# Grouping the mLSTM read-out by kind of matmul, and summing the dense feed-forward on VectorE with the residual at group 8

## The chip, the cores and the metric

The kernel runs on one core of one Trainium2 chip. The metric is the device time of one execution in microseconds (us); the time before is the median of three runs. TensorE multiplies matrices out of SBUF into PSUM, VectorE, ScalarE and GpSimd work on tiles element by element, and SyncE issues most transfers between HBM and SBUF. The engines run side by side, each through its own list of instructions in a fixed order, and wait for each other by semaphores.

## The reference

The model has two layers over 512 tokens (x) and 256 context tokens (ctx) of width 1024. Each layer mixes tokens by two recurrences side by side, HGRN2 and mLSTM, in both directions, and then applies a feed-forward: layer 0 a dense one, layer 1 a mixture of 8 experts of which each token takes two. A row `mod` of six modulation vectors comes from `w_ada`. Cut to what the change touches:

```python
# mLSTM, per chunk and head (one direction; both are summed)
s   = einsum("bhid,bhjd->bhij", qc, kc) * exp(d - m[..., None])
num = einsum("bhij,bhjv->bhiv", s, vc) + w_inter * einsum("bhid,bhdv->bhiv", qc, c_prev)
den = sum(s, -1) + w_inter[..., 0] * einsum("bhid,bhd->bhi", qc, n_prev)
h   = num / maximum(abs(den), exp(-m))[..., None]
...
# layer 0, feed-forward (D_FF = 2816), on x and on ctx
f = (silu(h @ w_gate) * (h @ w_up)) @ w_down
x = layer_norm(ALPHA * x + mod[:, 5] * f, ln_g, ln_b)
```

## The kernel before

Tokens lie on the 128 partitions: four tiles of x and two of ctx, together 768 tokens. Matmuls of weights run in a split form: each fp32 weight piece is loaded into a raw buffer (tag `wr`, two of them), ScalarE copies its rounded high part to `wh` (line 134), VectorE subtracts it and writes the low part `wl` (line 140, in the token mix shared with GpSimd in line 138), and `mm3` multiplies three times (lines 172 to 174). The activations have high and low parts as well (`xh`, `xl`, `hh`, `hl`).

**Read-out of the mLSTM.** The kernel's chunks have 128 tokens, ten passes over the two layers. For a chunk, line 726 makes scores of queries and keys (64 rows, since a head has 64 channels; even heads lie in rows 0 to 63, odd heads in 64 to 127), VectorE multiplies them by the decays into `W` (tile `tmp`), and the read-out adds for each of 4 heads and 2 directions the product of `W` with the values (line 736, 128 rows, 129 columns: the last column is the denominator) and the product of the queries with the state before the chunk (line 738, 64 rows). Both directions of a head share a PSUM tile of the tag "o", of which there are two; ScalarE copies a finished tile to `num` (line 739). These matmuls are in fp32, and the trace shows each as two records.

**Dense feed-forward of layer 0.** D_FF is cut into 11 groups of 256 columns, numbered 0 to 10. In each group the gate and up products are made in columns of hidden units, multiplied (line 865 and the lines behind it give `s`, `hh`, `hl`), and the down product of the six token tiles and two halves of 512 columns makes twelve PSUM tiles, in turn of the tags "o" and "sc", two buffers each. `evac` takes each of them into the accumulator `pre`: group 0 by a copy on ScalarE, each later one by a product with the modulation row `bd` on VectorE (line 1006) into a buffer `xm`, and a sum on GpSimd (line 1012). Groups 9 and 10 share one down product, so there is no evacuation at group 9; the last one sums on VectorE. In group 1, `evac` also multiplies what group 0 left by the row (line 1010) and adds the residual, which line 1009 loads from HBM into a buffer `xr` (line 1011). `xm` and `xr` take turns in four buffers of one tag. Between the groups, in groups 0 to 6, stand sums over `w_ada` for the next layer's modulation (lines 330 and 332: VectorE, pieces of 1024 columns that SyncE loads into `ar`).

The order on every engine is set when the program is built, by a scheduler that takes the instructions by priority as their inputs and buffers come free; names such as `o_1555` are its tiles.

Of the kernel before, what the change touches and what calls it, by code (L numbers as in the profile page):

```python
# [7 lines left out]
F32 = mybir.dt.float32  # L8
# [3 lines left out]
AF = mybir.ActivationFunctionType  # L12
OP = mybir.AluOpType
PSUM = bass.MemoryType.PSUM

P = 128
# [11 lines left out]
D_FF = 2816  # L28
# [21 lines left out]
class Kern:  # L50
# [483 lines left out]
    def mlstm(self, l, xh, xl, last):  # L534

        nc = self.nc
# [3 lines left out]
        for i in range(2):  # L540
            s = self.slot([3, 4, 129], True)
            nc.vector.memset(s[:, :, :, 128:129], 1.0)
            va.append(s)
        VA = lambda c: va[c // 3][:, c % 3]
        wmv = [self.w_cols(w, O_MV + 256 * half, 256) for half in range(2)]
        for t in range(NT):
            for half in range(2):
                p = self.gemm_T(wmv[half], xh, xl, t, 256)
# [8 lines left out]
        for f in range(2):  # L557
            for d in range(2):
                o = lambda t: t[:, :, 32 * f + 4 * d:32 * f + 4 * d + 4]
# [3 lines left out]
        for t0, n in ((0, TX), (TX, TC)):  # L563
            p = self.gemm_F((gh, gl), 0, 40, xh, xl, t0, n)
# [90 lines left out]
        for half, o in ((0, O_MQ), (1, O_MK)):  # L655
# [3 lines left out]
            for b in range(2):  # L659
                kcol = 2 * half + b  # L660
                for t0, n, seg in ((0, TX, 64), (TX, TC, TC)):
                    if last and half == 0 and t0:
                        continue
                    p = self.gemm_F(wqk, b * P, P, xh, xl, t0, n)
# [12 lines left out]
        st = lambda d, c: inc[c // 3][:, c % 3, 2 * d:2 * d + 2]  # L677
        for c in range(NT):
# [7 lines left out]
            for d in range(2):  # L686
# [3 lines left out]
                for hd in range(4):  # L690
                    b, s = hd // 2, hd % 2
                    nc.tensor.matmul(pc[64 * s:64 * s + 64, b], kw[:, d, hd], VA(c)[:, hd], start=True, stop=True)
                nc.scalar.activation(st(d, c), pc, AF.Copy)
        for i in range(1, NT - 1):
            for d in range(2):
                c, cp = ORDER[d][i], ORDER[d][i - 1]
# [3 lines left out]
        for c in (range(NX) if last else ORDER[0]):  # L700
            ds = [d for d in range(2) if POS[d][c] > 0]
# [5 lines left out]
            qs = self.s4([2, 2, P])  # L707
            for s in range(2):
                r = slice(64 * s, 64 * s + 64)
# [6 lines left out]
            W = M  # L716
# [4 lines left out]
            for s in range(2):  # L721

                pq = self.psum("sc", [P, 2, P])
                r = slice(64 * s, 64 * s + 64)
# [3 lines left out]
                    wv = W[:, d].rearrange("p (b s) t -> p b s t", s=2)[:, :, s]  # L728
                    nc.vector.tensor_tensor(wv, pq, wv, OP.mult)
            num = self.shp(self.sp.tile([P, 1032], F32, tag="num", name=self.nm("num"), bufs=2), [2, 4, 129])  # L730
            for hd in range(4):
                b, s = hd // 2, hd % 2
                r = slice(64 * s, 64 * s + 64)
                pn = self.psum("o", [P, 2, 129])
                for d in range(2):
                    nc.tensor.matmul(pn[:, d], W[:, d, hd], VA(c)[:, hd], start=True, stop=d not in ds)
                    if d in ds:
                        nc.tensor.matmul(pn[:, d], qs[r, d, b], st(d, ORDER[d][POS[d][c] - 1])[r, b], start=False, stop=True)
                nc.scalar.activation(num[:, :, hd], pn, AF.Copy)
            den = self.sp.tile([P, 2, 4], F32, tag="den", name=self.nm("den"), bufs=2)  # L740
            dv = num[:, :, :, 128]
            nc.vector.scalar_tensor_tensor(den, dv, -1.0, dv, op0=OP.mult, op1=OP.max)
# [161 lines left out]
    def run(self):  # L904
        nc, I, tc = self.nc, self.I, self.tc
# [23 lines left out]
        for l in range(DEPTH):  # L929
# [29 lines left out]
            for nqs in ((0,), (1,), (2, 3)):  # L959
# [4 lines left out]
                for t in range(nt):  # L964
                    for nq, w in zip(nqs, ww):
                        p = self.gemm_T(w, xh, xl, t, 256)
                        c = slice(nq * 256, nq * 256 + 256)
# [31 lines left out]
            def evac(t, half, p, g, end):  # L999
                c = slice(512 * half, 512 * half + 512)  # L1000
                o, bd = pre[:, t, c], bc5[t // NX][:, c]
                if g == 0:
                    nc.scalar.activation(o, p, AF.Copy)
                    return
                m = self.lp.tile([P, 512], F32, tag="xr", name=self.nm("xm"), bufs=4)
                nc.vector.tensor_tensor(m, p, bd, OP.mult)  # L1006
                if g == 1:
                    xr = self.lp.tile([P, 512], F32, tag="xr", name=self.nm("xr"), bufs=4)
                    nc.sync.dma_start(xr, self.xd[t * P:(t + 1) * P, c])
                    nc.vector.tensor_tensor(o, o, bd, OP.mult)  # L1010
                    nc.vector.scalar_tensor_tensor(o, xr, ALPHA, o, op0=OP.mult, op1=OP.add)
                (nc.vector if end else nc.gpsimd).tensor_tensor(o, o, m, OP.add)  # L1012

            def finish(t):
                self.finish(pre[:, t], self.stats(pre[:, t]), self.xd[t * P:(t + 1) * P], gb)
# [556 lines left out]
        return O, Wt  # L1572


PREP = 3
STREAMS = ((0, 1, 2), (6, 3, 7, 4, 5))
LEAD = 0.95
# [5 lines left out]
ORDER = ([4, 5, 0, 1, 2, 3], [5, 4, 3, 2, 1, 0])  # L1583
POS = [{c: i for i, c in enumerate(o)} for o in ORDER]
# [22 lines left out]
```

## Time and profile before

| | us |
|---|---|
| three runs | 2311.2, 2299.89, 2292.64 |
| median | 2299.89 |
| the profiled execution | 2313.89 |
| its span in the trace | 2312.1 |
| TensorE busy in it | 2093.4 (91%) |
| VectorE busy | 1530.9 (66%) |
| ScalarE busy | 912.4 (39%) |
| GpSimd busy | 526.8 (23%) |

The rows quoted further down are of the profiled execution, with times from the start of its span. The granted clock of TensorE (PEclk) is a share of its full 2.4 GHz; its mean over the span was 0.947. The first layer's token mix comes first, the dense feed-forward runs from about 640 to 1220 us, then come the second layer's token mix and its experts.

### The profile page before, as it was taken

To read this page: it belongs to the slowest core of one execution; us is meant where nothing else is said; L and a number is where in the kernel's file an instruction comes from. 1 tells how busy PE (TensorE), PEld (TensorE's weight loads), DVE (VectorE), ACT (ScalarE), POOL (GpSimd) and SP (SyncE) were. 2 spreads that over 40 slices of the span, in tenths; PEclk is the share of its full clock that TensorE was granted. 3 is DMA by queue.
4 is the path that set the end of the run, shared out by engine and by line. 5 is a ranking of instruction groups with operands and counts; after the bars stand their busy time and mean duration, and the time that the engine had idled before them with its cause. 6 is when DMAs were issued, how large, how long until landed. Compare 5 with 4: busy or idle time off the path is not lost. (4 is left out here: it accounts for less than half of the span.)

```text
span 2312.1 us, 32153 instructions
## 1 busy us (share of the span) xinstructions
PE 2093.4 (91%) x12225; PEld 1771.5 (77%) x12225; DVE 1530.9 (66%) x2527; ACT 912.4 (39%) x1443; POOL 526.8 (23%) x389
## 2 busy tenths in 40 slices
PE   8999999897799999999997999999979899798991
PEld 3887688897777777888886887889967787576781
DVE  4374684858977877544338366867669677776774
ACT  3334333344332221121124345334337565765661
POOL 1111312324621334443308112222220000000003
PEclk9998999998999999999998999999969999899996
DMA  7121311246354565222122222122558778888885
GB/s 256 39 87 43 118 44 44 71 143 202 128 161 145 174 191 158 65 64 64 55 68 75 61 77 69 42 60 80 205 181 296 237 266 280 264 282 274 280 283 133
DMA packets 232360, 333.38 MB, mean 144 GB/s; under 512 B 14608, under 2 KB 181716, under 8 KB 232200
## 3 DMA queue, kind: packets, MB, share of 16 engines
q1 hardware_dynamic: 228504, 319.14, 42.8%
q0 software_dynamic: 3696, 12.13, 2.1%
q8 instruction: 98, 1.61, 0.3%
q14 instruction: 62, 0.51, 0.1%
HBM read 305.98 MB, written 25.24 MB: 143 GB/s over the span
## 5 line engine op out<-in xcount | busy, mean ns | idle before, releaser
L173 PE MATMUL g<-xl,wh 128*128 128x512 f32 (+1 forms) x1168 | 402.1, 344 | 5.5 <-DVE xl L391 5.5
L174 PE MATMUL g<-xh,wl 128*128 128x512 f32 (+1 forms) x1168 | 401.7, 344 | 2.8 <-DVE wl L140 2.8
L172 PE MATMUL g<-xh,wh 128*128 128x512 f32 (+1 forms) x1168 | 402.7, 345 | 1.2 <-DVE s L865 0.9
L134 ACT ACTIVATE wh<-wr 128x1024 fp32r<-128x1024 f32 x240 | 249.2, 1055 | 253.5 <-PE sc L174 102.5
L172 PE MATMUL g<-wh,xh 128*128 128x256 f32 x1024 | 299.4, 293 | 19.6 <-DVE pre L968 11.2
L173 PE MATMUL g<-wl,xh 128*128 128x256 f32 x1024 | 298.0, 292 | 4.9 <-DVE wl L138 3.2
L174 PE MATMUL g<-wh,xl 128*128 128x256 f32 x1024 | 295.5, 289 | 0.0
L140 DVE TENSOR_TENSOR wl<-wr,wh 128x1024 fp32r<-128x1024 f32 x176 | 233.3, 1340 | 66.6 <-ACT wh L134 57.3
L173 PEld LDWEIGHTS g<-xl,wh 128*128 128x128 f32 x1168 | 221.6, 190 | 33.2 <-DVE xl L391 6.0
L172 PEld LDWEIGHTS g<-xh,wh 128*128 128x128 f32 x1168 | 221.7, 190 | 30.3 <-DVE s L865 1.3
L174 PEld LDWEIGHTS g<-xh,wl 128*128 128x128 f32 x1168 | 221.6, 190 | 30.3 <-DVE wl L140 4.1
L1012 POOL TENSOR_TENSOR pre<-pre,xm 128x512 f32<-128x512 f32 x96 | 159.5, 1691 | 330.4 <-DVE xm L1006 229.1
L157 DVE TENSOR_TENSOR wl<-wr,wh 128x1024 fp32r<-128x1024 f32 x154 | 186.1, 1219 | 53.8 <-ACT wh L156 52.5
L172 PEld LDWEIGHTS g<-wh,xh 128*128 128x128 f32 x1024 | 199.0, 195 | 24.9 <-DVE pre L968 11.8
L173 PEld LDWEIGHTS g<-wl,xh 128*128 128x128 f32 x1024 | 198.7, 194 | 7.5 <-DVE wl L138 3.9
L174 PEld LDWEIGHTS g<-wh,xl 128*128 128x128 f32 x1024 | 198.4, 194 | 0.7 <-issue 0.6
L156 ACT ACTIVATE wh<-wr 128x1024 fp32r<-128x1024 f32 x154 | 161.2, 1055 | 76.1 <-DMA wr<-in_moe_w_gate_up 65.4
L138 POOL TENSOR_TENSOR wl<-wr,wh 128x384 fp32r<-128x384 f32 x64 | 90.5, 1424 | 328.3 <-ACT wh L134 293.4
L332 DVE SCALAR_TENSOR_TENSOR acc<-ar,cond,acc 128x1024 f32<-128x1024 f32 x77 | 115.9, 1516 | 28.6 <-DMA ar<-in_w_ada 28.6
L138 DVE TENSOR_TENSOR wl<-wr,wh 128x640 fp32r<-128x640 f32 x64 | 66.4, 1039 | 90.2 <-ACT wh L134 89.4
L865 DVE TENSOR_TENSOR s<-g,s 128x512 f32<-128x512 f32 (+1 forms) x44 | 24.4, 553 | 129.0 <-PE g L174 129.0
L866 ACT ACTIVATE hh<-s 128x512 fp32r<-128x512 f32 (+1 forms) x44 | 23.0, 523 | 185.6 <-DVE s L865 185.6
(480 smaller groups left out, 4377.5 us busy)
## 6 DMA issues: line engine op xcount, KB each, us to landing
wr<-in_moe_w_gate_up SPq DMA_DIRECT2D x176, 512.0 KB
wr<-in_moe_w_down SPq DMA_DIRECT2D x88, 512.0 KB
wr<-in_w_in SPq DMA_DIRECT2D x64, 512.0 KB
ar<-in_w_ada SPq DMA_DIRECT2D x64, 512.0 KB
wr<-in_ffn_w_gate_up SPq DMA_DIRECT2D x44, 512.0 KB
wr<-in_w_ada SPq DMA_DIRECT2D x32, 512.0 KB
wr<-in_ffn_w_down SPq DMA_DIRECT2D x22, 512.0 KB
wr<-in_w_out SPq DMA_DIRECT2D x16, 512.0 KB
```

Source lines behind the costliest of these rows:

```text
L134: nc.scalar.activation(fl(h), r, AF.Copy)
L138: eng.tensor_tensor(fl(lo)[:, sl], r[:, sl], fl(h)[:, sl].bitcast(F32), OP.subtract)
L140: nc.vector.tensor_tensor(fl(lo), r, fl(h).bitcast(F32), OP.subtract)
L156: nc.scalar.activation(v(h, u), r, AF.Copy)
L157: nc.vector.tensor_tensor(v(lo, u), r, v(h, u).bitcast(F32), OP.subtract)
L172: nc.tensor.matmul(out, ah, bh, start=(i == 0), stop=False)
L173: nc.tensor.matmul(out, ah, bl, start=False, stop=False)
L174: nc.tensor.matmul(out, al, bh, start=False, stop=(i == n - 1))
L332: nc.vector.scalar_tensor_tensor(o, wk, cs, o, op0=OP.mult, op1=OP.add)
L865: nc.vector.tensor_tensor(s, pu, s, OP.mult)
L866: nc.scalar.activation(hh[:, b, t0:t0 + n], s, AF.Copy)
L1012: (nc.vector if end else nc.gpsimd).tensor_tensor(o, o, m, OP.add)
```

## The change

Two edits. In the read-out, two heads of a pair (`s` = 0 and 1) are taken together: both PSUM tiles of the tag "o", first the four products with `W`, then the products with the state, those of the two halves of rows next to each other, then both copies. In the dense feed-forward, groups 1 to 8 add the PSUM tile to the accumulator on VectorE, without the row and without GpSimd; the row is multiplied in, and the residual loaded and added, once, in group 8 (`GRES`). The last evacuation (groups 9 and 10) multiplies by the row and sums on VectorE as before.

```diff
             num = self.shp(self.sp.tile([P, 1032], F32, tag="num", name=self.nm("num"), bufs=2), [2, 4, 129])
-            for hd in range(4):
-                b, s = hd // 2, hd % 2
-                r = slice(64 * s, 64 * s + 64)
-                pn = self.psum("o", [P, 2, 129])
-                for d in range(2):
-                    nc.tensor.matmul(pn[:, d], W[:, d, hd], VA(c)[:, hd], start=True, stop=d not in ds)
-                    if d in ds:
-                        nc.tensor.matmul(pn[:, d], qs[r, d, b], st(d, ORDER[d][POS[d][c] - 1])[r, b], start=False, stop=True)
-                nc.scalar.activation(num[:, :, hd], pn, AF.Copy)
+            for b in range(2):
+                pn = [self.psum("o", [P, 2, 129]) for _ in range(2)]
+                for s in range(2):
+                    for d in range(2):
+                        nc.tensor.matmul(pn[s][:, d], W[:, d, 2 * b + s], VA(c)[:, 2 * b + s], start=d == 0, stop=False)
+                for d in ds:
+                    for s in range(2):
+                        r = slice(64 * s, 64 * s + 64)
+                        nc.tensor.matmul(pn[s][:, d], qs[r, d, b], st(d, ORDER[d][POS[d][c] - 1])[r, b],
+                                         start=False, stop=d == ds[-1])
+                for s in range(2):
+                    nc.scalar.activation(num[:, :, 2 * b + s], pn[s], AF.Copy)
...
                 if g == 0:
                     nc.scalar.activation(o, p, AF.Copy)
                     return
-                m = self.lp.tile([P, 512], F32, tag="xr", name=self.nm("xm"), bufs=4)
-                nc.vector.tensor_tensor(m, p, bd, OP.mult)
-                if g == 1:
+                if end:
+                    m = self.lp.tile([P, 512], F32, tag="xr", name=self.nm("xm"), bufs=4)
+                    nc.vector.tensor_tensor(m, p, bd, OP.mult)
+                    nc.vector.tensor_tensor(o, o, m, OP.add)
+                    return
+                nc.vector.tensor_tensor(o, p, o, OP.add)
+                if g == GRES:
                     xr = self.lp.tile([P, 512], F32, tag="xr", name=self.nm("xr"), bufs=4)
                     nc.sync.dma_start(xr, self.xd[t * P:(t + 1) * P, c])
                     nc.vector.tensor_tensor(o, o, bd, OP.mult)
                     nc.vector.scalar_tensor_tensor(o, xr, ALPHA, o, op0=OP.mult, op1=OP.add)
-                (nc.vector if end else nc.gpsimd).tensor_tensor(o, o, m, OP.add)
...
+GRES = D_FF // 256 - 3
```

After the change the lines behind 739 have moved by five. What the scheduler makes of it shows in the order of the instructions.

TensorE, read-out of a chunk in layer 0, the first three heads before the change (`early`, `tmp`: operands of the product with `W`; `s`: the state):

```order
L736 MATMUL o_1555<-early_421,tmp_1525 128x129 [waits DMAHW0_49,DVE_49]
L738 MATMUL o_1555<-tmp_1209,s_207_1528 128x129
L736 MATMUL o_1555<-early_421,tmp_1525 128x129 [waits DMAHW1_49,DVE_49]
L738 MATMUL o_1555<-tmp_1209,s_207_1528 128x129
L736 MATMUL o_1561<-early_421,tmp_1525 128x129 [waits DVE_49]
L738 MATMUL o_1561<-tmp_1209,s_207_1528 128x129
L736 MATMUL o_1561<-early_421,tmp_1525 128x129 [waits DVE_49]
L738 MATMUL o_1561<-tmp_1209,s_207_1528 128x129
L736 MATMUL o_1567<-early_421,tmp_1525 128x129 [waits Activation_49]
```

The same place after it:

```order
L737 MATMUL o_1555<-early_421,tmp_1525 128x129 [waits DMAHW0_49,DVE_49]
L737 MATMUL o_1555<-early_421,tmp_1525 128x129 [waits DMAHW1_49,DVE_49]
L737 MATMUL o_1556<-early_421,tmp_1525 128x129 [waits DVE_49] x2
L741 MATMUL o_1555<-tmp_1209,s_207_1528 128x129
L741 MATMUL o_1556<-tmp_1209,s_207_1528 128x129
L741 MATMUL o_1555<-tmp_1209,s_207_1528 128x129
L741 MATMUL o_1556<-tmp_1209,s_207_1528 128x129
L726 MATMUL sc_1614<-slot_939,slot_1080 128x128 [waits PE_49]
L726 MATMUL sc_1614<-slot_939,slot_1080 128x128
L737 MATMUL o_1567<-early_421,tmp_1525 128x129 [waits Activation_49]
```

Products with `W` and with the state no longer alternate; the next pair's first product (`o_1567`) stands behind two score matmuls and waits for ScalarE's copies.

VectorE, evacuation of group 8 before the change (`bd`: the row; `wl_9434`: low part of group 9's gate weights):

```order
L1006 TENSOR_TENSOR xm_9320<-o_9313,bd_5650 128x512 [waits PE_49,Pool_49]
L1006 TENSOR_TENSOR xm_9330<-sc_9323,bd_5650 128x512 [waits PE_49,Pool_49]
L140 TENSOR_TENSOR wl_9434<-wr_9435,wh_9433 128x1024 [waits DMAHW3_49,Activation_49]
L1006 TENSOR_TENSOR xm_9340<-o_9333,bd_5650 128x512 [waits PE_49,Pool_49]
L1006 TENSOR_TENSOR xm_9350<-sc_9343,bd_5650 128x512 [waits PE_49,Pool_49]
L140 TENSOR_TENSOR wl_9434<-wr_9439,wh_9433 128x1024 [waits DMAHW4_49,Activation_49]
```

The end of the same evacuation after it:

```order
L1020 TENSOR_TENSOR pre_4520<-pre_4520,bd_5651 128x512 [waits DVE_49]
L1015 TENSOR_TENSOR pre_4520<-sc_9229,pre_4520 128x512 [waits PE_49]
L1021 SCALAR_TENSOR_TENSOR pre_4520<-xr_9225,pre_4520 128x512 [waits DMAHW3_49,DVE_49]
L1020 TENSOR_TENSOR pre_4520<-pre_4520,bd_5651 128x512 [waits DVE_49]
L140 TENSOR_TENSOR wl_9242<-wr_9243,wh_9241 128x1024 [waits Activation_49]
L1021 SCALAR_TENSOR_TENSOR pre_4520<-xr_9237,pre_4520 128x512 [waits DMAHW4_49,DVE_49]
```

The split of group 9's first gate weights has moved from behind the second operation of the evacuation to behind the last multiplication, and each evacuation now has three operations.

SyncE, loads around group 9 after the change; none of these loads of `xr` stood here before:

```order
L124 DMA wr_9243<-in_ffn_w_gate_up 128x4x256 [waits DMAHW1_49,DVE_49]
L124 DMA wr_9247<-in_ffn_w_gate_up 128x4x256 [waits DMAHW2_49,DVE_49]
L1019 DMA xr_9153<-xd 128x512 [waits DVE_49]
L1019 DMA xr_9165<-xd 128x512 [waits DVE_49]
L1019 DMA xr_9177<-xd 128x512 [waits DVE_49]
```

Eight such loads stand together between the two gate pieces and the up pieces of group 9; the other four have moved ahead of the feed-forward.

## Rows read from the trace of the kernel before

**Rows 1.** Busy us by stretch (start:end, length, each engine, PEclk, DMA, GB/s): read-out.

```profile
core 0: us, PE busy (x) PEld busy (x) DVE busy (x) ACT busy (x) POOL busy (x), PEclk, DMA share, GB/s
128.00:230.00 102.00, 98.95 (x615) 80.61 (x613) 57.44 (x143) 47.04 (x77) 13.29 (x11) 0.92 0.20 60
1340.00:1440.00 100.00, 98.84 (x643) 82.08 (x642) 69.64 (x161) 53.05 (x83) 17.50 (x15) 1.00 0.25 72
```

**Rows 2.** Busy us by stretch: feed-forward groups 1, 2, 3, 5 and 7.

```profile
733.20:798.10 64.90, 56.63 (x280) 44.74 (x279) 54.76 (x67) 11.28 (x16) 23.17 (x12) 0.96 0.58 185
798.10:859.20 61.10, 55.40 (x279) 45.35 (x279) 45.81 (x52) 11.75 (x16) 22.12 (x12) 0.95 0.58 184
859.20:915.30 56.10, 53.49 (x273) 43.90 (x272) 42.40 (x44) 10.71 (x15) 21.96 (x12) 0.98 0.54 166
967.50:1019.60 52.10, 52.05 (x274) 43.67 (x273) 27.75 (x35) 10.05 (x14) 19.10 (x12) 1.00 0.19 60
1070.00:1120.10 50.10, 50.10 (x266) 42.92 (x265) 21.88 (x27) 10.10 (x14) 18.05 (x12) 1.00 0.20 64
```

**Rows 3.** Timeline of TensorE (start, duration, engine, line, records): two read-outs.

```profile
159.38 0.71 PE L736 MATMUL o<-early,tmp 128*128 128x129 f32 x4
160.02 0.49 PE L738 MATMUL o<-tmp,s 64*128 64x129 f32 x2
...
1406.83 0.38 PE L736 MATMUL o<-early,tmp 128*128 128x129 f32 x2
...
1412.57 0.49 PE L736 MATMUL o<-early,tmp 128*128 128x129 f32 x2
1412.99 0.37 PE L738 MATMUL o<-tmp,s 64*128 64x129 f32 x1
1412.99 0.37 PE L726 MATMUL sc<-slot,slot 64*128 64x128 f32 x1
```

**Rows 4.** Timeline, end of one head (in brackets: idle before, and its releaser).

```profile
1407.98 0.49 PE L738 MATMUL o<-tmp,s 64*128 64x129 f32 x2
...
1408.39 0.49 PE L736 MATMUL o<-early,tmp 128*128 128x129 f32 x2
...
1408.56 0.39 ACT L739 ACTIVATE num<-o 128x258 f32<-128x258 f32 x1 [0.91 <-PE o L738]
...
1410.45 1.05 ACT L134 ACTIVATE wh<-wr 128x1024 fp32r<-128x1024 f32 x1
```

**Rows 5.** Timeline, evacuation of group 1.

```profile
747.26 0.69 DVE L1011 SCALAR_TENSOR_TENSOR pre<-xr,pre 128x512 f32<-128x512 f32 x1 [2.36 <-DMA xr<-xd]
...
749.81 0.50 PE L172 MATMUL sc<-wh,hh 128*128 128x512 f32 x1 [2.26 <-DVE xm L1006]
...
752.30 4.75 SPq L1009 DMA_DIRECT2D xr<-xd  x2
```

**Rows 6.** Timeline of VectorE, `w_ada` sums and splits in group 2.

```profile
815.96 2.38 DVE L332 SCALAR_TENSOR_TENSOR acc<-ar,cond,acc 128x1024 f32<-128x1024 f32 x1
...
829.75 2.61 DVE L332 SCALAR_TENSOR_TENSOR acc<-ar,cond,acc 128x1024 f32<-128x1024 f32 x2 [2.29 <-DMA ar<-in_w_ada]
...
855.02 2.35 DVE L140 TENSOR_TENSOR wl<-wr,wh 128x1024 fp32r<-128x1024 f32 x2
```

**Rows 7.** Timeline, end of group 2.

```profile
853.82 1.28 DVE L332 SCALAR_TENSOR_TENSOR acc<-ar,cond,acc 128x1024 f32<-128x1024 f32 x1 [0.46 <-DMA ar<-in_w_ada]
...
856.29 0.79 PE L173 MATMUL o<-wl,hh 128*128 128x512 f32 x1 [3.58 <-DVE wl L140]
```

**Rows 8.** Timeline, evacuation of group 8 and the next gate product.

```profile
1120.13 0.68 DVE L1006 TENSOR_TENSOR xm<-o,bd 128x512 f32<-128x512 f32 x1
...
1128.10 0.67 DVE L1006 TENSOR_TENSOR xm<-sc,bd 128x512 f32<-128x512 f32 x1
1128.69 0.68 DVE L1006 TENSOR_TENSOR xm<-o,bd 128x512 f32<-128x512 f32 x1
...
1134.60 0.40 PE L172 MATMUL g<-xh,wh 128*128 128x512 f32 x1
```

**Rows 9.** Busy us by stretch, around the end of group 2.

```profile
852.00:862.00 10.00, 6.42 (x18) 4.68 (x17) 9.10 (x12) 2.44 (x4) 2.09 (x1) 0.66 0.69 220
```

## The prediction

> **What bounds the kernel now.** I read the table of busy time by stretch first, for the stages that the change touches. In both stretches that hold the mLSTM read-out TensorE is busy for 98.95 of 102 us and 98.84 of 100 us, at a granted clock of 0.92 and 1.00, while VectorE and ScalarE have room [rows 1]. What TensorE saves there shows in the end almost in full.
>
> The dense feed-forward is the second place. The same table, cut from the first evacuation of one down product to that of the next, shows what a group costs: 50.1 us for a group without modulation work (1070.0), 52.1 us for one that also sums a 1024-column piece of `w_ada` on VectorE (967.5), but 64.9, 61.1 and 56.1 us for groups 1 to 3 [rows 2]. Against 52.1 these three are 12.8, 9.0 and 4.0 us late, 25.8 us together. In them VectorE is busy for 54.8, 45.8 and 42.4 us; in group 7 for 21.9 of 50.1. So groups 1 to 3 hang on VectorE or on what it waits for, groups 4 to 8 on TensorE alone with VectorE more than half idle.
>
> The third view is the timeline of TensorE in one read-out [rows 3]. State matmuls (64 rows, line 738) and weight matmuls (128 rows, line 736) alternate, and each step takes 0.41 us: 14 steps from 1406.83 to 1412.57. Where two weight matmuls follow each other (x4 records at 159.38) the pair and the change behind it take 0.64 us, until 160.02; without the 0.41 of the last that leaves 0.22 for a matmul followed by its own kind. A change between 128 and 64 rows thus costs 0.20 us. The third thing to see: at 1412.99 a state matmul of rows 64 to 127 and a score matmul of rows 0 to 63 start together, and both go on side by side.
>
> **The read-out, part by part.** No matmul, copy or VectorE operation is added or removed; only the order and two PSUM tiles held together are new. I counted in TensorE's order, over the ten chunks and their score matmuls, the changes between 128 and 64 rows: 148 before, 68 after. (It would be fewer if all weight matmuls of a pair stood together; the first pair of most chunks is still broken up, because its weights come one by one from VectorE.) 80 changes less at 0.20 us are 16.0 us [rows 3]. State matmuls of the two halves now stand next to each other 23 times; side by side each pair saves 0.22 us, 5.1 us. Some 1.5 us of overlap between a state and a score matmul, which today exists once in a chunk, goes. That makes 19.5 us.
>
> The trace says 0.20 us for a change of row grouping, and that is what the sum uses. The Trainium skill (TensorEngine Tiling (Array Packing), Key Properties) says that a change of tiling mode drains TensorE, and (TensorE: Matmul & The Clock Gate, Single matmul latency) puts the fixed part of a matmul that hides nothing at about 166 ns at full clock; by that figure 80 changes would give 13.3 us, an estimate, instead of 16.0.
>
> What is added is a wait. Both tiles of the tag "o" are now filled together, so the second pair of heads may not start before ScalarE has copied the first pair. A state matmul at 1407.98 ends at 1408.47, its copy runs from 1408.56 to 1408.95 [rows 4], and TensorE could go on at about 1409.0 where today it went on at 1408.39: 0.6 us, behind which everything on TensorE queues. The order puts score matmuls or matmuls of a projection in between in most chunks, worth 0.2 to 0.4 us, so I take 0.4 us for ten chunks, 4 us. If one split copy of ScalarE stands in front (1.05 us at 1410.45 [rows 4]), a chunk loses up to 1.6 us and nearly all is lost; nothing, if the matmuls in between cover it. Net 15.5 us; with a little for the 3% in which TensorE waits for others, **14 us gained** (bounds 4 and 19).
>
> **The feed-forward, groups 1 to 3.** The number of VectorE operations stays the same: one per evacuation, product or sum, with one PSUM and one SBUF operand either way, so I take the 0.60 us from start to start of line 1006 [rows 8] for the sum too. Twelve multiplications by the row leave group 0 and twelve residual sums leave group 1, with their loads. In group 1 one of these sums waited 2.36 us for its load on VectorE's queue, with TensorE waiting 2.26 us behind it for a PSUM tile at 749.81, and at 752.30 SyncE spent 4.75 us on two such loads, because their buffers wait for GpSimd; the loads of `w_ada` and of weights stand behind them [rows 5]. All this goes.
>
> The 96 sums on GpSimd go: 18 to 23 us in each group [rows 2]. GpSimd itself bounds nothing, but VectorE pays: a `w_ada` sum of 1024 columns took 2.38 us at 815.96 beside a GpSimd sum and 1.3 us without (two in 2.61), a weight split 1.2 (two in 2.35) [rows 6]. Some ten operations of each group meet such a sum, 5 us or more of VectorE a group. So VectorE's 54.8 us in group 1 falls by 8 for the residual and by 5, to about 42 of 52.
>
> I do not take all 25.8 us, for one wait has another cause. In group 2 VectorE stood behind `w_ada` loads (the last idled it 0.46 us); the split of the down weights came behind it in the fixed order, at 855.02, and TensorE waited 3.58 us [rows 6, 7]. The new order keeps that pattern: sums that each need a load, then the split. It also keeps what follows: in the 10 us around that wait the granted clock was 0.66, a mix of the two levels, 2.4 GHz and 1.2 [rows 9]. My choice: of 12.8, 9.0 and 4.0 us there remain 3, 6 and 2.5, **14 us gained** (bounds: 3, if the loads set the pace everywhere, and 25.8).
>
> **The feed-forward, group 8.** Here VectorE gets 24 more operations, and in its order the split of group 9's gate weights now stands behind the twelfth multiplication, where before two splits lay between the evacuations. Before: evacuation from 1120.13, TensorE at the next gate product by 1134.60 without a wait [rows 8]. After: 36 operations at 0.60 us are 21.6 us, to 1141.8, then a split of 1.2 us [rows 6], 1143.0. TensorE gets there at about 1134.6, can do two matmuls that need no split, and waits until 1143: 8 us. PSUM alone costs little, since each tile is free after the sum, one in three operations, and there are four. Eight of the twelve residual loads stand together on SyncE in front of group 9's up weights and wait for buffers of the sums before them; the up weights are needed only 24 gate matmuls after the gate split, so I price that at under 1 us. Four others move up to the end of layer 0's token mix, between loads that already wait for GpSimd: 0 to 2 us, within the range. A wait of 3.58 us was followed by a lower clock [rows 9], so I add 2 us. **10 us lost** (bounds 6, and 14 with 0.68 us an operation, as line 1006 takes alone, and a longer time at the low level).
>
> Nothing else changes in kind: the last group sums as before, and the expert stage runs the same code.
>
> **Sum.** -14 - 14 + 10 = -18 us. The profiled run took 2313.89 us (its span 2312.1), 14 us above the median of the runs shown; I take the difference from the median 2299.89: **2282 us**, or 2296 for a run like the profiled one. About 1% (23 us) is what a measurement here can tell from no change.
>
> **Rivals.**
> Full relief: VectorE's load was the whole cause in groups 1 to 3, with no late split left. 25.8 us instead of 14, and group 8 at 7: -14 - 25.8 + 7 = -33, 2267 us. For it: VectorE's busy time in these groups. Against: the waits for loads in rows 7.
> Read-out gain lost at the copies: the 0.6 us falls due in full and ScalarE is late in some chunks. -4 - 14 + 10 = -8, 2292 us. For it: only two tiles; against: in the new order of ScalarE the four copies of most chunks stand together.
> Slower: group 8 takes over the bound. From the point where the three operations of an evacuation together outlast the 1.32 us in which TensorE makes a tile (14.47 us for the eleven behind the first [rows 8]) by more than the four tiles cover, TensorE idles until the last multiplication; at 0.68 us an operation that is 11 us, and the clock falls for 7 us more, 14 us lost. With the loads still setting the pace in groups 1 to 3 (3 us gained) and 5 us from the read-out: +6, 2306 us.
> No effect: the scheduler keeps the old order. The order of the first chunk is indeed almost the old one, the others are not; 2300 us.
>
> **How the numbers follow.** Forecast 0.50, full relief 0.20, copies 0.15, slower 0.12, no effect 0.03. The range 2264 to 2303 takes in full relief and the copies and leaves out about 0.2, half of it with the slower case. Faster by over 1% (2277 or less): full relief and three tenths of the forecast, 0.35; slower by over 1%: a third of the slower case, 0.04; within 1%: 0.61.
>
> **What would show it.** In the profile after: weight matmuls in records of x4 or x8, state matmuls of two halves starting together, and no wait above 0.6 us for the read-out's copies. Groups 1 to 3 at 55, 58 and 55 us; no GpSimd sums; VectorE's 1024-column operations at 1.2 to 1.3 us. Group 8 to the next gate product: one wait of TensorE of 6 to 9 us for the split, and a lower clock behind it. The prediction is wrong if the split in group 8 comes earlier than its place in the order says, if ScalarE's copies come over a microsecond late, or if groups 1 to 3 do not move.

## The result, and the profile after

The changed kernel takes **2275.96 us** (median of six, 2272.68 to 2282.57) against 2299.97 (six, 2292.64 to 2311.2): ratio 0.9897, 95% interval [0.9869, 0.9925], 24 us less. Predicted were 2282 us and 18 less. Sent again on another chip it gave 0.9917 [0.989, 0.9945].

The profiled execution took 2273.86 us. TensorE lost 37 us of busy time, GpSimd 168:

```profile
PE 2056.1 (90%) x12225; PEld 1752.8 (77%) x12225; DVE 1498.9 (66%) x2527; ACT 909.0 (40%) x1441; POOL 358.8 (16%) x293
```

The busy time by stretch answers to [rows 2]: groups 1, 2 and 3, and group 8's evacuation to that of the last group.

```profile
720.40:777.20 56.80, 55.00 (x282) 45.18 (x280) 46.87 (x58) 11.78 (x16) 0.00 (x0) 0.97 0.58 184
777.20:832.60 55.40, 53.95 (x283) 44.31 (x282) 39.99 (x52) 11.98 (x16) 0.00 (x0) 1.00 0.63 203
832.60:883.20 50.60, 50.60 (x269) 42.86 (x268) 32.69 (x41) 10.99 (x15) 0.00 (x0) 1.00 0.47 153
...
1087.80:1189.00 101.20, 92.93 (x483) 78.07 (x482) 45.12 (x66) 20.28 (x28) 0.00 (x0) 0.97 0.27 86
```

The last stretch in the trace before:

```profile
1120.10:1212.30 92.20, 90.85 (x482) 76.79 (x481) 33.82 (x41) 20.19 (x28) 18.05 (x12) 1.00 0.24 71
```

Groups 1 to 3 together took 182.1 us and now take 162.8; the last stretch grew from 92.2 to 101.2. Group 1 begins at 720.4 in place of 733.2, which is the token mix with its six read-outs; part of this is the granted clock, as told further down.

The timeline of TensorE and ScalarE in the last read-out of layer 1 answers to [rows 3] and [rows 4]:

```profile
1398.41 0.71 PE L737 MATMUL o<-early,tmp 128*128 128x129 f32 x4
1399.06 0.71 PE L741 MATMUL o<-tmp,s 64*128 64x129 f32 x6
1399.65 0.66 ACT L744 ACTIVATE num<-o 128x258 f32<-128x258 f32 x2 [0.67 <-PE o L741]
1399.69 0.39 PE L172 MATMUL g<-xh,wh 128*128 128x256 f32 x1
...
1400.15 1.11 PE L737 MATMUL o<-early,tmp 128*128 128x129 f32 x8
1401.19 0.72 PE L741 MATMUL o<-tmp,s 64*128 64x129 f32 x8
1401.83 0.39 PE L172 MATMUL g<-xh,wh 128*128 128x256 f32 x1
```

Four weight matmuls (x8 records) go from 1400.15 to 1401.19, four state matmuls from 1401.19 to 1401.83: 1.68 us for a pair of heads, where eight steps of 0.41 made 3.3. The next pair's first weight matmul starts at 1400.15, while ScalarE's two copies run to 1400.31; three matmuls of a projection stand in between. In the stretches with read-outs no wait of TensorE's matmuls for these copies is listed; its weight loads waited for them four times, 1.1 us in all.

The end of group 8's evacuation answers to [rows 8]:

```profile
1087.77 0.68 DVE L1015 TENSOR_TENSOR pre<-o,pre 128x512 f32<-128x512 f32 x1
...
1102.46 0.40 PE L173 MATMUL g<-xl,wh 128*128 128x512 f32 x1
...
1108.31 0.69 DVE L1020 TENSOR_TENSOR pre<-pre,bd 128x512 f32<-128x512 f32 x1
1108.91 1.22 DVE L140 TENSOR_TENSOR wl<-wr,wh 128x1024 fp32r<-128x1024 f32 x1
...
1110.19 0.80 PE L174 MATMUL g<-xh,wl 128*128 128x512 f32 x1 [7.33 <-DVE wl L140]
```

VectorE runs through the evacuation without a pause from 1087.77, the split follows at 1108.91 behind 35 of the 36 operations, and TensorE waits 7.33 us for it. Behind that the granted clock is 0.68 for 7 us with TensorE busy throughout:

```profile
1110.20:1117.20 7.00, 7.00 (x21) 5.59 (x22) 2.93 (x4) 2.12 (x2) 0.00 (x0) 0.68 0.48 151
```

### The profile page after: what moved, and what is told of

Read it like the earlier page. It is cut to its first block, busy times and chain, and to the rows that moved or that the text cites. A ratio compares the mean times of both kernels' runs of the same rounds, so it can differ in the third digit from the quotient of the medians.

```text
span 2272.1 us, 31952 instructions
## 1 busy us (share of the span) xinstructions
PE 2056.1 (90%) x12225; PEld 1752.8 (77%) x12225; DVE 1498.9 (66%) x2527; ACT 909.0 (40%) x1441; POOL 358.8 (16%) x293
## 5 line engine op out<-in xcount | busy, mean ns | idle before, releaser
L140 DVE TENSOR_TENSOR wl<-wr,wh 128x1024 fp32r<-128x1024 f32 x176 | 216.0, 1242 | 70.6 <-ACT wh L134 66.0
L157 DVE TENSOR_TENSOR wl<-wr,wh 128x1024 fp32r<-128x1024 f32 x154 | 186.1, 1219 | 49.3 <-ACT wh L156 47.7
L138 POOL TENSOR_TENSOR wl<-wr,wh 128x384 fp32r<-128x384 f32 x64 | 85.2, 1342 | 362.7 <-ACT wh L134 358.2
L332 DVE SCALAR_TENSOR_TENSOR acc<-ar,cond,acc 128x1024 f32<-128x1024 f32 x77 | 107.1, 1406 | 36.4 <-DMA ar<-in_w_ada 36.4
L847 POOL TENSOR_TENSOR r<-r,mhalf 128x1 f32<-128x1 f32 x20 | 14.1, 706 | 622.2 <-DVE r L846 622.2
```

What stands on the lines that cost most here:

```text
L138: eng.tensor_tensor(fl(lo)[:, sl], r[:, sl], fl(h)[:, sl].bitcast(F32), OP.subtract)
L140: nc.vector.tensor_tensor(fl(lo), r, fl(h).bitcast(F32), OP.subtract)
L157: nc.vector.tensor_tensor(v(lo, u), r, v(h, u).bitcast(F32), OP.subtract)
L332: nc.vector.scalar_tensor_tensor(o, wk, cs, o, op0=OP.mult, op1=OP.add)
L847: nc.gpsimd.tensor_tensor(r, r, self.mhalf[:, 0:1], OP.pow)
```

## The experiments

All ratios are to the kernel before on the same chip.

**1. The read-out alone.** The diff is the first part of the change; the feed-forward is the old one.

> The kernel before with the grouped read-out alone; the feed-forward is the old one. Theory (each change between 128 and 64 rows costs 0.20 us, and the wait for the copies is covered by score matmuls): the ten read-outs get 17 us shorter, ratio to before 0.992 to 0.9935, and the feed-forward groups 1 to 3 stay at about 65, 61 and 56 us. Rival (the second pair of heads waits for the first pair's copies): 8 us or less, ratio 0.9965 or more. Rival (the shorter read-out seen in the changed kernel's trace was a matter of the clock, which fell in one read-out of the trace before): under 5 us.

Measured: 2291.91 us against 2305.4, ratio 0.994 [0.9921, 0.9958], 14 us less. Groups 1 to 3 of its feed-forward are as slow as before:

```profile
726.10:789.90 63.80, 56.53 (x281) 44.60 (x280) 54.53 (x67) 11.39 (x16) 23.19 (x12) 0.97 0.59 188
789.90:849.40 59.50, 54.22 (x279) 44.26 (x278) 45.75 (x52) 11.76 (x16) 22.11 (x12) 0.98 0.62 190
849.40:906.60 57.20, 53.58 (x273) 43.69 (x273) 42.98 (x45) 10.70 (x15) 21.91 (x12) 0.99 0.52 162
```

So the feed-forward's gain does not come from an earlier start. The two rivals of under 8 and under 5 us are out; the theory's 17 lies in the interval, which reaches from 10 to 18, though the ratio lies just over its band.

**2. The feed-forward alone.** The diff is the second part of the change.

> The kernel before with the new feed-forward alone; the read-out is the old one. Theory (groups 1 to 3 gain 19 us, the stall for the weight split behind group 8 gives 9 back): 10 us less, ratio 0.9945 to 0.9965, groups 1 to 3 at 57, 55 and 51 us, and a wait of TensorE of about 8 us after group 8's down products. Rival (what the two traces show in groups 1 to 3 hangs on the earlier start that the read-out gives, or on the run): under 5 us, ratio above 0.998.

Measured: 2298.84 us, 0.9968 [0.9953, 0.9983], 7 us less; groups 1 to 3 at 56.9, 56.0 and 50.7 us, the last stretch 101.5, with the same wait. Its stages are those of the theory; its total lies just over the theory's band. Both parts add up to 21 us, within the interval of the whole.

**3. The residual behind group 9.** Group 9 has no evacuation. Lines 1019 to 1021 become a function that is called behind its products:

```diff
                 nc.vector.tensor_tensor(o, p, o, OP.add)
-                if g == GRES:
...
+            def residual(t, half):
+                c = slice(512 * half, 512 * half + 512)
+                o, bd = pre[:, t, c], bc5[t // NX][:, c]
+                xr = self.lp.tile([P, 512], F32, tag="xr", name=self.nm("xr"), bufs=4)
+                nc.sync.dma_start(xr, self.xd[t * P:(t + 1) * P, c])
+                nc.vector.tensor_tensor(o, o, bd, OP.mult)
+                nc.vector.scalar_tensor_tensor(o, xr, ALPHA, o, op0=OP.mult, op1=OP.add)
...
+                if g == GRES + 1:
+                    for t in tiles:
+                        for half in range(2):
+                            residual(t, half)
```

> The changed kernel with the row multiplication, the residual load and the residual sum taken out of group 8's evacuation and written behind group 9's gate and up products, where no evacuation stands; same operations, same sums. Theory (the wait of 7.7 us behind group 8 is the split queued behind the residual operations, and nothing else): the wait goes, from group 8 to the end takes 92 us in place of 101, ratio to before 0.985 to 0.987 (2267 us). Rival (the loads of the residual hold up the weight loads on SyncE wherever they stand, or the last group then waits for the late residual): the stall appears in group 10 instead, no gain against the changed kernel (0.9897).

Measured: 2278.95 us, 0.9892 [0.9876, 0.9909], over the theory's band. Its last stretch took 92.0 us, as forecast, but the total told nothing, since the changed kernel had run on another chip. Therefore both once more, side by side.

> The changed kernel as it is, once more, as the neighbour on the same chip of the three runs sent with it: ratio to before 0.988 to 0.992, a wait of TensorE of 7.7 us behind group 8.

> The kernel with the residual behind group 9's products again, now beside the changed kernel on one chip. Its first run had no wait behind group 8 (92 us to the end in place of 101), yet its ratio to before was only that of the changed kernel on another chip. Theory (the 9 us are real and were hidden by the spread from chip to chip and run to run): 7 to 10 us under the changed kernel of this call. Rival (what is saved there is given back in a later stage): no difference from the changed kernel, over 0.997 of it, with a later stage that is longer in both of its traces.

Measured: 2287.63 us and 0.9917 for the changed kernel, 2272.98 and 0.9864 [0.9832, 0.9896] with the residual behind group 9: 15 us less, more than the 9 of the stall, though the two intervals overlap. The stretch of the last groups, and group 1 ahead of it:

```profile
721.10:778.80 57.70, 55.04 (x283) 45.39 (x282) 46.91 (x59) 11.67 (x16) 0.00 (x0) 0.97 0.58 181
...
1091.80:1183.70 91.90, 90.74 (x483) 76.74 (x482) 44.99 (x66) 20.19 (x28) 0.00 (x0) 1.00 0.30 94
```

VectorE still does the work of the changed kernel in that stretch (44.99 us, 45.12 there), and the split runs between the first evacuations, at 1094.38. In the changed kernel ScalarE had copied the piece to be split at 1089.15, 19 us before VectorE came to it, so the wait was the queue on VectorE.

**4. VectorE sums with the residual at group 1.** One line, `GRES = 1`. The modulation row is left out for the products of groups 2 to 8, so the operations are as many as in the changed kernel. Twelve multiplications by the row now stand in group 1 that the kernel before ran in group 0 (line 1010, 696.6 to 716.6). The experts then work on other values, and the total (2523.7 us) says nothing here; only the feed-forward is compared.

> The changed kernel with the row multiplication and the residual at group 1 again, and VectorE sums as in the changed kernel. Left out: the modulation row on groups 2 to 8, whose products are added without it, so the numbers of operations stay those of the changed kernel. It tells apart what relieved groups 1 to 3. Theory (the residual's waits and operations made most of group 1, GpSimd's sums beside VectorE most of groups 2 and 3): group 1 at 61 to 65 us, groups 2 and 3 at 55 and 51 as in the changed kernel, group 8 to the end 92 us; ratio 0.987 to 0.990. Rival (the residual loads in group 1 also push back the loads of w_ada and so made groups 2 and 3 late): groups 1 to 3 at 63, 60 and 55 us, ratio 0.992 or more. Rival (only GpSimd mattered): group 1 at 57, ratio 0.985.

Measured, groups 1 to 3 and the last stretch:

```profile
719.70:787.40 67.70, 56.61 (x280) 45.72 (x279) 58.81 (x80) 11.50 (x16) 0.00 (x0) 0.93 0.53 169
787.40:846.80 59.40, 56.15 (x290) 45.94 (x289) 42.57 (x54) 12.12 (x17) 0.00 (x0) 0.99 0.64 203
846.80:896.10 49.30, 49.30 (x263) 41.76 (x262) 33.22 (x41) 10.58 (x15) 0.00 (x0) 1.00 0.51 162
1100.70:1192.50 91.80, 90.83 (x483) 76.74 (x482) 31.10 (x42) 20.19 (x28) 0.00 (x0) 1.00 0.24 71
```

Group 1 is slower than with the old sums and than the theory's 61 to 65, and its timeline shows group 8's stall in the same form: the next group's gate split behind the operations of the evacuation.

```profile
742.43 1.22 DVE L140 TENSOR_TENSOR wl<-wr,wh 128x1024 fp32r<-128x1024 f32 x1
...
743.70 0.80 PE L174 MATMUL g<-xh,wl 128*128 128x512 f32 x1 [6.67 <-DVE wl L140]
```

With three operations in each evacuation the stall came in both places where these stood. Group 2 is 4 us late too, which the theory had not expected (its rival had); group 3 is not.

**5. GpSimd sums with the residual behind group 9.** The grouped read-out and the old sums; line 1010, the row on group 0's part, stays in group 1, and the residual's load and sum go where experiment 3 has them.

> The grouped read-out with the old feed-forward sums (product on VectorE, sum on GpSimd, row multiplication of group 0's part in group 1), but the residual's load and sum moved behind group 9's products: the fourth corner beside the kernel with the old feed-forward, the one with VectorE sums and the residual at group 1, and the one with VectorE sums and the residual behind group 9. Theory (in group 1 the residual's operations and loads cost most, in group 3 the GpSimd sums beside VectorE): group 1 at 58 to 61 us, group 2 at 58 to 60, group 3 still at 56 to 57; operations of VectorE over 1024 columns still 1.5 us in the mean, as before. Rival (the sums on GpSimd made group 1 too): group 1 at 63 or more. Rival (GpSimd costs nothing): groups 1 to 3 at 57, 55 and 51.

Measured: 2293.88 us, 0.9949 [0.993, 0.9967]. Groups 1 to 3:

```profile
723.10:787.10 64.00, 55.85 (x282) 45.17 (x281) 53.07 (x59) 11.42 (x16) 20.47 (x12) 0.97 0.52 162
787.10:849.90 62.80, 55.50 (x278) 44.56 (x277) 45.99 (x52) 11.76 (x16) 21.04 (x12) 0.93 0.57 181
849.90:904.10 54.20, 52.47 (x274) 43.94 (x273) 37.90 (x42) 10.81 (x15) 21.36 (x12) 0.99 0.44 141
```

The first rival was right: 64.0 us in group 1. Taking the residual's loads and sums away from group 1 gives nothing while GpSimd sums. What GpSimd costs VectorE stands in the groups of instructions of groups 1 to 3 (busy us, mean ns), first before, then after the change:

```profile
L332 DVE SCALAR_TENSOR_TENSOR acc<-ar,cond,acc 128x1024 f32<-128x1024 f32 x41 | 60.9, 1490 | 22.6 <-DMA ar<-in_w_ada 22.5
L140 DVE TENSOR_TENSOR wl<-wr,wh 128x1024 fp32r<-128x1024 f32 x18 | 26.6, 1492 | 0.9 <-ACT wh L134 0.7 <-PE g L174 0.3
```

```profile
L332 DVE SCALAR_TENSOR_TENSOR acc<-ar,cond,acc 128x1024 f32<-128x1024 f32 x41 | 52.1, 1281 | 27.8 <-DMA ar<-in_w_ada 27.8
L140 DVE TENSOR_TENSOR wl<-wr,wh 128x1024 fp32r<-128x1024 f32 x18 | 21.5, 1219 | 1.7 <-ACT wh L134 1.7
```

The four corners, as the sum of groups 1 to 3: old sums with the residual at group 1, 180.5 (experiment 1); old sums with it behind 9, 181.0; VectorE sums with it at 1, 176.4; VectorE sums with it behind 9, 166.1. Each edit alone is worth 0 or 4 us, both together 14. The corners are not clean, though: experiment 4 has the stall of 6.67 us, and in experiment 5 a matmul of the modulation (line 344) waits 4.8 us for VectorE in group 2; in the kernel before the waits at these two places were 1.3 us or less. They show that neither edit alone, as written here, relieves these groups, and not how much of the old delay each cause made.

**6. The read-out by heads.** Two weight matmuls, two state matmuls, one tile, copy; the feed-forward of the changed kernel.

```diff
-            for b in range(2):
-                pn = [self.psum("o", [P, 2, 129]) for _ in range(2)]
...
+            for hd in range(4):
+                b, s = hd // 2, hd % 2
+                r = slice(64 * s, 64 * s + 64)
+                pn = self.psum("o", [P, 2, 129])
+                for d in range(2):
+                    nc.tensor.matmul(pn[:, d], W[:, d, hd], VA(c)[:, hd], start=d == 0, stop=False)
+                for d in ds:
+                    nc.tensor.matmul(pn[:, d], qs[r, d, b], st(d, ORDER[d][POS[d][c] - 1])[r, b], start=False, stop=d == ds[-1])
+                nc.scalar.activation(num[:, :, hd], pn, AF.Copy)
```

> The changed kernel with the read-out in order of heads: two weight matmuls, then two state matmuls, one PSUM tile at a time, copy; the pair is not taken together. Theory (the price is 0.20 us for each change between 128 and 64 rows, and adjacent halves save 0.22 us a pair): a read-out of 8 heads-by-direction has 8 changes in place of 16, so it takes 6.5 - 1.6 = 4.9 us in place of 6.5 before, and the changed kernel is about 1.3 us shorter still by four changes less and by the halves side by side, counted without the score matmuls in between; in all 10 us less than the old order in the read-outs and 5 to 9 more than the changed one. Rival (only the halves side by side matter): near 6.5 us, as before. Rival (the second tile's wait for the copy eats the rest): as short as the changed kernel or shorter.

Measured: 2297.7 us, 0.9969 [0.9948, 0.999], 10 us more than the changed kernel on the same chip. Its timeline:

```profile
1416.91 0.71 PE L736 MATMUL o<-early,tmp 128*128 128x129 f32 x4
1417.55 0.71 PE L738 MATMUL o<-tmp,s 64*128 64x129 f32 x4
1418.19 0.71 PE L736 MATMUL o<-early,tmp 128*128 128x129 f32 x4
```

Two matmuls and a change take 0.64 us; a whole read-out without the clock falling takes 5.13 us (248.2 to the next matmul) against the 6.68 of the one at 254.4 before: 1.55 for eight changes, 0.19 each. In the changed kernel four state matmuls of the two halves take the same 0.64 as two of one half here. Both prices hold in these rows. The gain over the changed kernel's order lies just above the 5 to 9 us expected, and in the profiled execution the clock fell in two read-outs (8.92 and 9.64 us); how much of the 10 us that is stays open. The total does not show the 10 us that this order should save against the old one: 0.9969 here, 0.9968 in experiment 2, where the old order stands beside the same feed-forward.

**7. What is left in groups 1 and 2.** Three attempts on the kernel of experiment 3. The first writes `between(g)` behind the loads of the down weights:

> The kernel with the residual behind group 9, and with the w_ada sums of a group written behind the loads and splits of its down weights in place of ahead of them; same operations. Theory (what is left of the delay in groups 1 and 2 is the split of the down weights queued on VectorE behind sums that wait for their loads): the waits of 2.2 and 1.4 us for that split go, groups 1 and 2 at 53 to 54 us, another 4 us less than the kernel with the residual behind group 9 (ratio to before 0.984 to 0.987). Rival (the loads themselves are late: weights and w_ada share SyncE's queue): the waits stay or move to the modulation columns, no gain.

Measured: 0.9877 [0.9843, 0.9911], groups 1 to 3 at 57.2, 57.6 and 53.0 us. VectorE's order had stayed as it was at the split, for the scheduler places by what is ready, so this tested nothing. The second lowers the sums' priority:

```diff
+                    p0 = self.tc.cur_priority
+                    self.tc.cur_priority = p0 + 400
                     self.ada_vec(j, m, self.lp, 2 if j == 0 or m < 2 else 1)()
+                    self.tc.cur_priority = p0
```

> The kernel with the residual behind group 9, and the w_ada sums of a group given a lower priority by 400 instructions, which in VectorE's order takes the next group's first two w_ada sums out from in front of the split of group 1's down weights; the earlier attempt, writing the sums later in the code, had left that order as it was. Same operations. Theory (the wait of 2.2 to 3.1 us for the split of the down weights in group 1 is the split queued behind a sum that waits for its load): that wait falls under 1 us, group 1 at 54 to 55 us in place of 57, ratio to before 0.984 to 0.987. Rival (the down weights' own load and rounding are late as well, since SyncE issues them behind the w_ada loads): the wait stays at 1.5 us or more, no gain, ratio as the kernel without it (0.9864 and 0.9892).

Measured: 0.9886 [0.9863, 0.991], no gain. In group 1 the wait for the split fell from 2.7 to 0.3 us, and the group to 55.0 as forecast; groups 0 and 6 paid for it (51.4 and 50.5 us in the kernel without the edit):

```profile
669.10:723.90 54.80, 53.82 (x278) 44.37 (x277) 32.24 (x35) 18.69 (x28) 0.00 (x0) 1.00 0.48 156
723.90:778.90 55.00, 53.65 (x277) 44.06 (x276) 43.09 (x49) 12.09 (x16) 0.00 (x0) 1.00 0.47 150
...
991.30:1045.60 54.30, 53.69 (x279) 43.97 (x278) 23.14 (x38) 10.09 (x14) 0.00 (x0) 1.00 0.19 58
```

The third parts the two double vectors of the next layer (16 operations each); a third one, of layer 0, stays first:

```diff
-            todo = [(0, 5)] + [(1, m) for m in (1, 0, 2, 3, 4, 5)]
+            todo = [(0, 5)] + [(1, m) for m in (2, 1, 3, 0, 4, 5)]
...
-                if g == 3:
+                if g == 5:
```

> The kernel with the residual behind group 9, and the seven w_ada vectors of groups 0 to 6 in another order: the two that are summed for x and ctx both (16 sums of 1024 columns each) no longer follow each other in groups 1 and 2, but stand in groups 2 and 4 with single ones around them; what hangs on them (the affine columns) moves from group 3 to group 5. Same operations. Theory (groups 1 and 2 are late since VectorE is busy for over 42 us of a group in a row and its splits of the down weights fall behind; one light group between lets it catch up): groups 1 to 4 together at 208 to 212 us in place of 218, ratio to before 0.984 to 0.987. Rival (each of the heavy groups is late by itself, whatever stands around it): 5 us late in group 2 and 4 each, groups 1 to 4 at 216 to 219 us, no gain, ratio 0.986 to 0.9895.

Measured: **2270.33 us, 0.984 [0.9812, 0.9868]**, the fastest version, under both kernels. Groups 1 to 4:

```profile
730.20:782.10 51.90, 51.90 (x273) 43.60 (x272) 30.47 (x37) 11.29 (x16) 0.00 (x0) 1.00 0.46 146
782.10:834.90 52.80, 52.80 (x281) 44.17 (x280) 40.98 (x55) 11.64 (x16) 0.00 (x0) 1.00 0.44 137
834.90:887.50 52.60, 52.60 (x277) 43.92 (x276) 30.57 (x37) 11.24 (x16) 0.00 (x0) 1.00 0.43 143
887.50:940.30 52.80, 52.80 (x281) 44.16 (x280) 32.39 (x46) 11.56 (x16) 0.00 (x0) 1.00 0.36 118
```

TensorE is busy in all of it, and no wait is left in these groups: 210.1 us for the four in place of 218.3. About half of that is given back ahead of them: TensorE waits 2.9 us for the split of group 0's down weights, where the kernel without the edit has no such wait, and group 0 takes 53.0 us in place of 51.4. The four groups have less to do, too: 35 sums of line 332 fall into them, where 41 fell into groups 1 to 3. In group 2 a double vector between single ones causes no wait; in the old order three stand in a row, and what two in a row would do no run shows. The ratio's interval overlaps that of 0.9864, from another chip, so the step from experiment 3 to this one is not shown on the total.

**8. The same order with the old feed-forward.** The same two lines in the kernel of experiment 1.

> The grouped read-out with the old feed-forward (sums on GpSimd, row and residual at group 1), and the w_ada vectors in the interleaved order, with the two double ones in groups 2 and 4. Theory (the delay of groups 1 to 3 is a backlog of VectorE, and GpSimd's sums and the residual only lengthen it where two double vectors follow each other): groups 2 to 4 at 53 to 55 us in spite of the GpSimd sums, group 1 at 56 to 60 with the residual's operations and waits, groups 1 to 4 together 220 to 226 in place of the 232.7 of the grouped read-out alone, ratio to before 0.989 to 0.992. Rival (the VectorE sums and the late residual are what relieves these groups, and the order of the vectors counts only on top of that): groups 1 to 4 at 228 us or more, ratio 0.992 or more.

Measured, groups 1 to 4:

```profile
722.90:781.20 58.30, 54.22 (x274) 43.00 (x273) 42.86 (x50) 11.06 (x16) 17.92 (x12) 1.00 0.57 183
781.20:835.10 53.90, 53.13 (x282) 44.21 (x281) 46.57 (x56) 11.51 (x16) 21.89 (x12) 1.00 0.43 136
835.10:890.30 55.20, 53.24 (x277) 43.67 (x276) 37.06 (x37) 11.15 (x16) 21.43 (x12) 1.00 0.43 134
890.30:945.50 55.20, 53.29 (x281) 44.14 (x280) 37.45 (x46) 11.66 (x16) 21.52 (x12) 1.00 0.36 114
```

222.6 us, inside the theory's band, 10 under the 232.7 without the edit. The total disagrees: 2290.43 us, 0.9944 [0.9927, 0.9962], no better than experiment 1. The profiled execution (2282.17 us) was, with one of 2282.11, the fastest of twelve, and which of the others had this gain no trace shows. So the order of the vectors is shown to shorten the stage in one trace with either kind of sums, and the total with neither.

## Why the prediction was right

**Read-out: forecast 14, the stages show 19.** In the eleven traces with the grouped read-out group 0's first evacuation comes at 668.4 to 677.2 us, in the mean 672.0; with the old one at 681.8 and 684.7. That is 11.3 us for six read-outs, 1.9 each, but part of it is the clock. In both traces with the old order it fell in the second and the fourth read-out, in the fourth of the trace before at 215.95, where a step grows from 0.42 to 0.73 us:

```profile
215.53 0.49 PE L738 MATMUL o<-tmp,s 64*128 64x129 f32 x2
215.95 0.80 PE L736 MATMUL o<-early,tmp 128*128 128x129 f32 x2
216.68 0.80 PE L738 MATMUL o<-tmp,s 64*128 64x129 f32 x2
```

These two read-outs took 5.88 and 9.43 us at a granted clock of 0.71 and 0.63, where the others of layer 0 took 4.89 and 6.38 to 6.72 at 0.96 or more: some 4 us of the 11.3, an estimate from these durations. In the eleven traces the clock was at 1.00 in both and low in the sixth instead (5.29 to 8.02 us at 0.88 to 0.53). Whether that goes with the order no run shows. In layer 1 the four read-outs span 66.5 us before and 58.3 after, 2.0 each, at a clock of 1.00 in all eight. The gross sum of 19.5 agrees with the stages, and layer 1's part of it is clear of the clock; the 0.20 us for a change was taken a little high, for the rows give 0.18 (0.64 less 0.41 leaves 0.23, not 0.22) and experiment 6 gives 0.19. The step that failed is the added wait of 0.4 us a read-out: the order puts score or projection matmuls between the pairs, and they cover the copies but for 1.1 us of weight loads in ten read-outs. Experiment 1's total shows less, 14 us; in its trace the clock fell in two read-outs (7.8 and 6.2 us in place of 5.3 and 4.7), 4 us in all. Whether that is the whole difference stays open, and that it equals the net forecast does not speak for the wait.

**Groups 1 to 3: forecast 14, measured 16.** 181.3 us in the two traces with the old feed-forward and order, 165.3 in the mean of the seven with the new sums, the residual at 8 or 9 and the old order of vectors. Groups 1 to 3 remained 4.7, 3.3 and -1.5 us over 52.1 in the profiled execution, where I had 3, 6 and 2.5. That the split of the down weights behind the `w_ada` sums stays late was right: TensorE's waits for it went from 6.8 to 3.0 us, and in these groups only parting the double vectors took all of them away. The division was wrong, and that the sum came this near is in part luck: I had summed 8 us of VectorE for the residual and 5 for GpSimd's sums, as if they added up, to leave VectorE busy for 42 us in group 1; it was busy for 46.9. Over three groups of 52.1 us the delay was 24 us in experiment 1 and still 20 and 25 in experiments 4 and 5, with one of the two left in place, though each with a wait of its own. GpSimd's share of VectorE was 209 ns on each of 41 sums and 273 on each of 18 splits, 13.5 us over three groups, somewhat under the 5 us or more a group that I had put on some ten operations.

**Group 8: forecast 10 lost, measured 9.** 101.2, 101.5, 101.2 and 100.4 us where the residual stands in group 8, 92.2 and 92.5 before. The wait was 7.33 us for the forecast 8; the 35 operations ahead of the split took 21.1 us (1087.77 to 1108.91); the forecast 21.6 counted all 36, though in the order that it read the last stands behind the split. The lower clock behind it came as the rows of before had it. The rival in which this stall decides had the right mechanism, but the gains beside it were larger than it allowed; the rival of the copies fell with the wait that did not come, and the full relief of 25.8 us with the split that stayed late.

**Sum.** 19 + 16 - 9 is 26 us by stages, 24 by the medians, 18 forecast. The profiled executions differ by 40. Of the rest 8 lie behind layer 1's last read-out, where the code is the same and where the stretch took 870 to 881 us in all traces but experiment 4's: spread, not the change.

## What to carry to other kernels

Where an engine is saturated, as TensorE is in the read-out, count the changes of its mode in the order of instructions; the price of one, read off a place where it is absent, forecast the gain of a read-out at full clock (1.95 us, 2.0 in layer 1); the total of experiment 1 moved by 14 us, not 19. Work that is moved to an idle engine's slack still stands in that engine's queue: look which instruction that another engine waits for comes behind it, and move the work to where no such instruction follows. Several causes that fill one backlog need not add up: here taking away the residual's loads and sums alone gave nothing. The order of the heavy pieces counts as well, but look beside the stage that gains, too: about half of its 8 us was given back just ahead of it.

## What the hardware showed that I had not expected

Beside GpSimd's sums VectorE's operations with both tensor inputs in SBUF took 1490 and 1492 ns (lines 332 and 140), without them 1281 and 1219 (1387 and 1570 in experiment 5, where GpSimd sums and the residual is away); the 128x512 operations that read one input from PSUM took 680 ns beside GpSimd and 684 without. The Trainium skill (GPSIMD Engine Reference, 1. Specifications) has this rule: GpSimd shares its SBUF interfaces with VectorE and contends with VectorE instructions that have two SBUF inputs. The rows agree.

The two halves of rows ran side by side not only for one pair of matmuls, as in [rows 3], but for four in a row: x8 records in 0.64 us against x4 in 0.64 for one half. That different tiles can compute in parallel is what the Trainium skill says (TensorEngine Tiling (Array Packing), Key Properties); the trace agrees.

The same read-out of the same kernel ran at different granted clocks in different executions:

```profile
242.90:248.60 5.70, 5.70 (x37) 4.58 (x36) 2.29 (x3) 1.81 (x4) 1.65 (x2) 0.87 0.65 187
```

```profile
246.00:254.50 8.50, 8.50 (x37) 6.83 (x36) 2.80 (x5) 1.90 (x4) 2.63 (x2) 0.54 0.45 126
```

Both are the sixth read-out of the changed kernel, of its first and of its second profile, 37 records each. In both, TensorE had stood still twice just ahead, for a weight copy (1.9 and 2.0 us) and for the modulation row (1.6 and 1.4), and the clock was at its lower level; in the first it rose early in the read-out, by 244.40, in the second only near its end, before the last four state matmuls at 253.92. What decides this is not shown. Such read-outs, 1.5 to 4.5 us longer, came in ten of the fourteen traces and are part of the spread between executions.
